# q and k in products of 512 columns, a smaller step of side work beside them, and a third Strassen piece in the second down product

## The chip, the cores and the metric

The kernel runs on one core of a Trainium2 chip. The metric is the device time of one execution in microseconds (us). The engines have short names in the profile: PE is TensorE's matrix products and PEld its weight loads (they overlap), DVE is VectorE, ACT is ScalarE, POOL is GpSimd, SP is SyncE, from whose queue the large loads are started.

## The reference, cut to what matters

One decoder layer on a sequence of 256 tokens with 1024 channels, all in float32:

```
h = h + 0.5 * rmsnorm(swiglu(rmsnorm(h)))                 # FFN 1: 1024 -> 2816 -> 1024
u = rmsnorm(h)
z, xbc, dt_raw, q, k, v, gate_logits = split(u @ w_in)
y_ssd = ssd_branch(z, xbc, dt_raw)                        # Mamba-2: conv, 2 chunks of 128, gated norm, @ ssd_w_branch
y_att = diff_attn_branch(q, k, v)                         # 8 heads, two softmaxes each, norm, @ da_w_branch
h = h + rmsnorm((gates[0] * y_ssd + gates[1] * y_att) @ w_out)
h = h + 0.5 * rmsnorm(swiglu(rmsnorm(h)))                 # FFN 2, of the same form
```

with `swiglu(x) = (silu(x @ w_gate) * (x @ w_up)) @ w_down`. Of q, k and v, head h has q and k as two halves of 64 channels and one v of 128; its output is `softmax(q0 k0) v - lam * softmax(q1 k1) v`, normed over its 128 channels.

## The kernel before

**Products in three terms.** Operands are split into two parts that TensorE multiplies in one pass each: hi (a cast by ACT) and lo (what is left, a subtraction by DVE). A product is hi x hi + hi x lo + lo x hi, so each weight chunk costs ACT a cast and DVE a subtraction per 1024 columns (`split_steps`, L249 and L252), and TensorE three matmuls per block of 128 x 128.

**Weights.** All weights arrive as chunks of 1 MB through a ring of three buffers (`raw`, loads from SP's queue at L228). A buffer's next load is issued when the chunk in it has been split. `take()` hands out the next chunk and has the splits of up to three chunks ahead put into the program. The split parts, and most other large tiles, share a pool of 29 buffers of 4 KB per partition (`k4`); a smaller one (`k3`) has four.

**Forms of a product.** `mm_t` (L293) gives 256 output channels by 256 tokens in one PSUM tile: 48 matmuls of 256 columns. `mm_w` (L305) gives the same in two tiles of 128 channels; hi weights multiply the hi and lo activations at once, 512 columns, lo weights the hi activations, 256 columns: 16 matmuls of each kind. ACT then copies one half of the tile and DVE adds the other (L318, L319). Gate and up of both FFNs use `mm_w`; B, C, x, z, q and k of the mixer use `mm_t`. `natural` (L1352) is the form with tokens on the partitions: per chunk two groups of 12 matmuls of 512 columns, one for each block of 128 tokens. PSUM tiles of products come from a ring of three (`pj`).

**Down product.** `mm_quads` sums the hidden layer in pieces. A plain piece `p` is one chunk of 256 hidden channels, 24 matmuls of 512 columns. A piece `q` is two chunks by Strassen's algorithm (in Winograd's form): seven products of six matmuls where two plain pieces have 48 matmuls. Four of its seven weight operands are sums that DVE forms (`Quad.sum_of`, L121), each of the seven is then cast (L129) and subtracted (L134); `sums_of` (L603 and on) forms the activation sums while gate and up still run. `DOWN` gives the order of pieces, the digit being the pair of chunks; `FIRST` and `LAST` the order of the seven products in all `q` but the last, and in the last. When the last `q` is through, four additions (L649) combine the Strassen sums, and the three plain pieces at the end are done block by block (`mm_n`, L568), so that the first block's norm lies beside the second block's products.

**Side work of the mixer.** SSD steps and attention are written as generators that yield after each step with a cost in us that is written by hand. `Background.run(us)` adds `us` to a due time and emits steps until it is used up, or until a step yields `BREAK`. The calls stand between the products of the projections: `run(0.4)` after each x chunk, `run(BG_US)` with 3.15 after each z, q and k chunk, `run(GATE_US)` (1.35) after each group of 12 gate products (`pgt`), `run(SSD_US)` (1.55) after each group of the SSD branch product (`pws`) and of the first half of the attention branch product (`pwd`). The queue holds, one behind the other, the causal B-C products, four SSD groups, four SSD norms (their sum over channels is the two matmuls `pn`), and attention.

Attention goes by pairs of heads. A step of it emits scores (`psc`, L1161), softmax (L1168 and on), the turns of the pair before (`pa`, L1196), its values (`po`, L1208 to L1210), its norm (square on ACT L1222, reduction on DVE L1224, root on ACT, scaling on DVE L1229), and the turn of the normed output of the pair before that (`pto`, L1235), whose hi and lo parts (L1247, L1248) are the operands of `pwd`. Before `pwd` begins, steps are emitted until pairs 0 and 1 are turned; after the first chunk of `pwd`, `attended` emits all that is left.

**Order.** From the gate products on, TensorE's instructions stand in the order in which they are written (`own_order(PE)`); the order on ACT and DVE there, and on all engines in the projections and in gate and up, comes from a scheduler. Each engine takes its instructions in order, and the loads of SP's queue are started in order.

Of the kernel before, what the change touches and what calls it, by code (L numbers as in the profile page):

```python
# [17 lines left out]
F32R = mybir.dt.float32r  # L18
AF = mybir.ActivationFunctionType
ALU = mybir.AluOpType  # L20
# [6 lines left out]
P = 128  # L27
T = 256
# [13 lines left out]
FILL = 2  # L42
TAIL = 3
BG_US = 3.15
GATE_US = 1.35
SSD_US = 1.55
DOWN = {"f1": "p q1 p p q2 p ppp", "f2": "p q1 p p q2 p ppp"}
FIRST, LAST = (1, 2, 3, 5, 7, 6, 4), (1, 6, 7, 2, 5, 3, 4)
BREAK, STOP = object(), object()

# [2 lines left out]
def tile_hybrid_layer(ctx: ExitStack, tc: tile.TileContext, x, ffn1_pre_g, ffn1_w_gate, ffn1_w_up,  # L53
# [4 lines left out]
    nc = tc.nc  # L58
# [5 lines left out]
    def k4(shape, name, dt=F32):  # L64
        return sb.tile(shape, dt, tag="k4", name=name, bufs=K4_BUFS)

    def k3(shape, name, dt=F32):
        return sb.tile(shape, dt, tag="k3", name=name, bufs=K3_BUFS)

    def k2(shape, name, dt=F32):  # L70
        return sb.tile(shape, dt, tag="k2", name=name, bufs=K2_BUFS)
# [7 lines left out]
    def pj(name):  # L79

        return ps.tile([P, 512], F32, tag="pj", name=name, bufs=3)

    def pjt(name):

        return pj(name).rearrange("p (m t) -> p m t", m=2)

    def bg(shape, name):
        return ps.tile(shape, F32, tag="bg", name=name, bufs=5)
# [3 lines left out]
    class Quad:  # L92
# [32 lines left out]
        def split(self, p):  # L125
            load_to(self.i + 2)
            hi = k4([P, 2, 512], f"wqh{self.i}{p}", F32R)
            src = self.quarter(self.PLAIN[p], p) if p in self.PLAIN else self.sum_of(p)
            nc.scalar.copy(hi, src)  # L129
            for later in self.products[self.products.index(p) + 1:][:1]:  # L130
                if later in self.SUMS:
                    self.sum_of(later)
            lo = k4([P, 2, 512], f"wql{self.i}{p}", F32R)
            last_lo[0] = nc.vector.tensor_sub(lo, src, hi.bitcast(F32)).ins  # L134
            self.give_back()
            return lambda kt: hi[:, kt, :], lambda kt: lo[:, kt, :]
# [28 lines left out]
    down, QUADS = {}, {}  # L165
    for tag, plan in DOWN.items():
        QUADS[tag] = [int(c) for c in plan if c.isdigit()]
# [90 lines left out]
    def split_to(n):  # L258

        while len(splits) < min(n, len(units)):  # L260
            of, p = units[len(splits)]
            if p is not None:
                splits.append(of.split(p))
                continue
            for _ in split_steps():
                pass

    def ahead_of(i, n):

        n *= 4  # L270
        while n > 0 and i < len(units):
            n -= 4 if units[i][1] is None else 1
            i += 1
        return i

    def take(ahead=AHEAD):

        i = taken[0]
        taken[0] += 1
        split_to(ahead_of(i, ahead))  # L280
        (of, p), w = units[i], splits[i]
        splits[i] = None
        if p is not None:
            return w
        his, los = w
        nj = chunks[of][1][1] // 2
        return (lambda j: his[j // nj][:, j % nj, :], lambda j: los[j // nj][:, j % nj, :])
# [5 lines left out]
    def mm_t(acc, w, act, k0=0, first=True, last=True, ks=range(KD)):  # L293

        (wh, wl), (ah, al, _) = w, act
        acc = acc if isinstance(acc, list) else [acc[:, m, :] for m in range(2)]
        for m in range(2):
            cs = slice(m * P, (m + 1) * P)
            for j in ks:
                nc.tensor.matmul(acc[m], wh(j)[:, cs], ah(k0 + j), start=first and j == ks[0], stop=False)  # L300
                nc.tensor.matmul(acc[m], wh(j)[:, cs], al(k0 + j), start=False, stop=False)  # L301
            for j in ks:
                nc.tensor.matmul(acc[m], wl(j)[:, cs], ah(k0 + j), start=False, stop=last and j == ks[-1])

    def mm_w(dst, name, w, act):  # L305


        (wh, wl), (ah, _, ahl) = w, act
        for m in range(2):
            acc = pj(f"{name}{m}")  # L310
            cs = slice(m * P, (m + 1) * P)
            for j in range(KD):
                if j:
                    nc.tensor.matmul(acc[:, :T], wl(j)[:, cs], ah(j), start=False, stop=False)  # L314
                nc.tensor.matmul(acc, wh(j)[:, cs], ahl(j), start=j == 0, stop=j == KD - 1)  # L315
                if not j:
                    nc.tensor.matmul(acc[:, :T], wl(j)[:, cs], ah(j), start=False, stop=False)
            nc.scalar.copy(dst[:, m, :], acc[:, T:])  # L318
            nc.vector.tensor_tensor(dst[:, m, :], acc[:, :T], dst[:, m, :], ALU.add)  # L319

    def mm_nat(acc, w, act, k0, first, last, late):

# [26 lines left out]
    def act_table(name):  # L349
        f = nc.scalar.preload_act_table_set(name)  # L350
        for prev in act_since:
            tc.add_manual_dep(f.ins, prev, order, reason="activation table")
        act_since.clear()
        act_fence[0] = f.ins.name
# [61 lines left out]
    for name, v in (("mx", mix_pre_g), ("f2", ffn2_pre_g),  # L416
                    ("ng", ssd_norm_g), ("cb", ssd_conv_b), ("sg", da_subln_g)):
        n = v.shape[1] // P
# [7 lines left out]
    def new_u(tag):  # L426
        for i in range(2):
            uT[i] = sb.tile([P, 4, 2, T], F32R, tag="u8", name=f"u{i}_{tag}", bufs=2)

    act_u = (lambda j: uT[j // 4][:, j % 4, 0, :], lambda j: uT[j // 4][:, j % 4, 1, :],  # L430
             lambda j: uT[j // 4][:, j % 4, :, :])
# [163 lines left out]
    def sums_of(g, even, odd):  # L595


        bs = (slice(0, P), slice(P, T))
        v = k4([P, 4, 2, P], f"sv{g}")
        hi, lo = (k3([P, 3, 2, P], f"s{n}{g}", F32R) for n in "hl")  # L600
        more = k2([P, 2, 2, P], f"s4{g}", F32R)
        nc.vector.tensor_tensor(v[:, 0], even[:, :, bs[1]], odd[:, :, bs[1]], ALU.add)
        nc.vector.tensor_sub(v[:, 2], even[:, :, bs[0]], even[:, :, bs[1]])  # L603
        nc.vector.tensor_sub(v[:, 1], v[:, 0], even[:, :, bs[0]])
        nc.vector.tensor_sub(v[:, 3], odd[:, :, bs[0]], v[:, 1])
        split(hi, lo, v[:, 0:3])
        split(more[:, 0], more[:, 1], v[:, 3])
        return ([hi[:, i] for i in range(3)] + [more[:, 0]], [lo[:, i] for i in range(3)] + [more[:, 1]])
# [417 lines left out]
    for i in range(4):  # L1026
        acc = pjt(f"pbc{i}")
        mm_t(acc, take(), act_u)
        dst = (bT, cT)[i // 2]
# [111 lines left out]
    qT = [None] * 2  # L1141
    kT = [None] * 2
# [167 lines left out]
    back = Background()  # L1310
    back.add(cb_work())
    for g in range(4):
        xs[g] = k4([P, 4, T], f"xs{g}")
        for i in range(2):
            acc = pjt(f"pxs{g}{i}")
# [5 lines left out]
    for g in range(4):  # L1321
        sz[g] = k4([P, 4, T], f"sz{g}")
        for i in range(2):
            acc = pjt(f"pz{g}{i}")
            mm_t(acc, take(), act_u)
            nc.scalar.copy(sz[g][:, i * 2:i * 2 + 2, :], acc)
            back.run(BG_US)
    act_table(SILU)
# [4 lines left out]
    for c in range(4):  # L1333
        if c % 2 == 0:
            qT[c // 2] = k4([P, 4, T], f"q{c}")
            kT[c // 2] = k4([P, 4, T], f"k{c}")
        o = (c % 2) * 2
        acc = pjt(f"pq{c}")
        mm_t(acc, take(), act_u)
        nc.scalar.activation(qT[c // 2][:, o:o + 2, :], acc, AF.Copy, scale=0.125)  # L1340
        back.run(BG_US)
        acc = pjt(f"pk{c}")
        mm_t(acc, take(), act_u)
        nc.scalar.copy(kT[c // 2][:, o:o + 2, :], acc)
        back.run(BG_US)

    back.add(att_work())

# [3 lines left out]
    def natural(name, n, hi, lo, evict, us, then=lambda: None):  # L1352


        accs = [pj(f"{name}{b}") for b in range(2)]
        for i in range(n):
            w = take()
            for b in range(2):
                bs = slice(b * P, (b + 1) * P)
                mm_nat(accs[b], w, (lambda k: hi(k)[:, bs], lambda k: lo(k)[:, bs]), i * 4, i == 0, i == n - 1, "u")  # L1360
                if i == n - 1:
                    evict(b, accs[b])
                back.run(us)
            if i == 0:
                then()
# [9 lines left out]
    for half in range(2):  # L1375
# [4 lines left out]
        for q in range(2):  # L1380
            def gate(b, acc):
                nc.vector.tensor_tensor(gt[half][b][:, halves[q]], acc, gb[:, halves[q]], ALU.add)

            natural(f"pgt{half}{q}", 2, uh, ul, gate, GATE_US)
    opens.append(open_gates)
# [42 lines left out]
    acc = [[bg([P, 512], f"acc_mx{b}{q}") for q in range(2)] for b in range(2)]  # L1428
# [47 lines left out]
```

## Time and profile before

| | us |
|---|---|
| median of 3 runs (lowest to highest) | 739.85 (739.61 to 741.19) |
| the profiled execution | 740.56 |
| its span, first to last instruction | 738.9 |
| DVE's most costly group: lo parts of weights (L252) | 271.1 in 230 instructions |
| ACT's: hi parts of weights (L249) | 229.9 in 229 |
| matmuls of gate and up, 512 columns (L315) | 2 x 288 instructions |
| q and k products, on PE | from 344.7 to 398.0 |
| down product of FFN 2, on PE | from 674.24 to 732.0 |

In rows of grouped instructions stand line, engine, operation, output <- inputs, sizes, count, then busy time and the mean of one in ns, and the idle time ahead of them with what ended it. In the timeline's rows stand start, duration in us, engine, line, operation, names and count; in brackets the idle time ahead and what ended it. In rows by stage, each engine has its busy time and, in parentheses, its number of instructions; then the granted TensorE clock, the share of the DMA engines and GB/s.

### The profile page before, as it was taken

The numbers are of one execution on the slowest core, as the hardware profiler recorded it, in microseconds if no ns is written. First come the engines' busy times: TensorE is split into PE (matmuls) and PEld (weight loads), VectorE is DVE, ScalarE is ACT, GpSimd is POOL, SyncE is SP. The second block draws the span as 40 slices with busy tenths as digits, with TensorE's granted clock in tenths as the row PEclk, the third lists the DMA queues.
The fourth block names the chain that finished last, engine by engine and source line by source line (L and its number), as shares of the span: only waits on it lengthen the run. The fifth ranks groups of instructions, "written<-read, shape, count | busy, mean of one in ns | idle before, by whom it ended". The sixth has DMA issues, their size and how long they took to land.

```text
span 738.9 us, 11097 instructions
## 1 busy us (share of the span) xinstructions
PE 729.9 (99%) x4345; PEld 637.2 (86%) x4345; DVE 576.5 (78%) x875; ACT 456.1 (62%) x764; POOL 38.8 (5%) x72
## 2 busy tenths in 40 slices
PE   8999999999999999999999999999999999999996
PEld 7888888888889999999999888888888888888884
DVE  6978768998677888777878997685784878768964
ACT  6657556665566565959957656782663656656542
POOL 2700000000300000000000000000010000000000
PEclk9999999999999999999999999999999999999998
DMA  8884674469353647566556556475471764843641
GB/s 291 234 256 150 221 229 171 159 201 355 119 172 116 202 140 231 187 192 220 172 162 213 168 175 211 126 237 190 127 238 35 228 206 152 270 170 128 214 143 57
DMA packets 94212, 137.96 MB, mean 187 GB/s; under 512 B 2684, under 2 KB 68304, under 8 KB 94160
## 3 DMA queue, kind: packets, MB, share of 16 engines
q1 hardware_dynamic: 91488, 129.51, 53.8%
q0 software_dynamic: 2368, 7.22, 3.2%
q8 instruction: 34, 0.56, 0.3%
q10 hardware_dynamic: 304, 0.53, 0.2%
q14 instruction: 18, 0.15, 0.1%
HBM read 136.17 MB, written 1.08 MB: 186 GB/s over the span
## 4 chain that ended last, share of the span: by engine, by line
PE 99%; DMA 0%; DVE 0%; ACT 0%; DVEq 0%; issue 0%
PE pup_f L315 9%; PE pg_f L315 9%; PE pws L330 6%; PE pgt L330 6%; PE acc_f2p L620 5%; PE acc_f1p L620 5%; PE pg_f L314 4%; PE pup_f L314 4%; PE pn_f L340 3%; PE pn_f L330 3%; PE acc_mx L568 3%; PE pn_mx L330 3%; PE pwd L330 3%; PE acc_f1p L568 3%; PE acc_f2p L568 3%; PE pz L301 2%
## 5 line engine op out<-in xcount | busy, mean ns | idle before, releaser
L252 DVE TENSOR_TENSOR wlo<-raw,whi 128x1024 fp32r<-128x1024 f32 (+1 forms) x230 | 271.1, 1209 | 27.3 <-ACT whi L249 26.0
L249 ACT CAST whi<-raw 128x1024 fp32r<-128x1024 f32 (+1 forms) x229 | 229.9, 1044 | 24.4 <-PE pgt L330 5.8
L315 PE MATMUL pg_f<-u_f,whi 128*128 128x512 f32 x288 | 101.3, 396 | 0.0
L315 PE MATMUL pup_f<-u_f,whi 128*128 128x512 f32 x288 | 101.1, 396 | 0.0
L314 PE MATMUL pg_f<-u_f,wlo 128*128 128x256 f32 x252 | 70.6, 280 | 0.0
L314 PE MATMUL pup_f<-u_f,wlo 128*128 128x256 f32 x252 | 70.3, 279 | 0.0
L315 PEld LDWEIGHTS pg_f<-u_f,whi 128*128 128x128 f32 x288 | 52.8, 188 | 9.7
L315 PEld LDWEIGHTS pup_f<-u_f,whi 128*128 128x128 f32 x288 | 52.7, 188 | 9.8
L314 PEld LDWEIGHTS pg_f<-u_f,wlo 128*128 128x128 f32 x252 | 47.5, 189 | 1.8
L314 PEld LDWEIGHTS pup_f<-u_f,wlo 128*128 128x128 f32 x252 | 47.5, 189 | 1.6
L319 DVE TENSOR_TENSOR su_f<-pup_f,su_f 128x256 f32<-128x256 f32 x36 | 15.1, 421 | 26.7 <-ACT su_f L318 26.7
L318 ACT COPY su_f<-pup_f 128x256 f32<-128x256 f32 x36 | 13.3, 371 | 32.7 <-PE pup_f L315 32.6
L330 PE MATMUL pgt<-whi,u_mx 128*128 128x512 f32 x128 | 33.1, 393 | 0.0
L300 PE MATMUL pxs<-u_mx,whi 128*128 128x256 f32 x128 | 31.7, 285 | 0.0
L301 PE MATMUL pz<-u_mx,whi 128*128 128x256 f32 x128 | 31.7, 284 | 0.0
L300 PE MATMUL pz<-u_mx,whi 128*128 128x256 f32 x128 | 31.6, 284 | 0.0
L301 PE MATMUL pxs<-u_mx,whi 128*128 128x256 f32 x128 | 31.4, 283 | 0.0
L129 ACT CAST wqh<-wt 128x1024 fp32r<-128x1024 f32 x16 | 16.8, 1052 | 23.5 <-DVE wt L121 22.3
L330 PEld LDWEIGHTS pgt<-whi,u_mx 128*128 128x128 f32 x128 | 23.6, 188 | 5.4 <-DVE yl L291 0.3
L1004 DVE SCALAR_TENSOR_TENSOR xs<-pxs,cols_b,xs 128x255 f32<-128x255 f32 (+2 forms) x48 | 21.9, 476 | 6.3 <-ACT xs L1001 5.9
L301 PEld LDWEIGHTS pz<-u_mx,whi 128*128 128x128 f32 x128 | 24.5, 192 | 0.2 <-issue 0.2
L301 PEld LDWEIGHTS pxs<-u_mx,whi 128*128 128x128 f32 x128 | 24.5, 192 | 0.0
(395 smaller groups left out, 1677.2 us busy)
## 6 DMA issues: line engine op xcount, KB each, us to landing
raw<-in_w_in_dram SPq DMA_DIRECT2D x40, 1024.0 KB, 5.5
raw<-in_ffn_w_down_dram SPq DMA_DIRECT2D x22, 1024.0 KB, 5.0
raw<-in_ffn_w_gate_dram SPq DMA_DIRECT2D x20, 1024.0 KB, 5.6
raw<-in_ffn_w_up_dram SPq DMA_DIRECT2D x20, 1024.0 KB, 5.5
raw<-in_ssd_w_branch_dram SPq DMA_DIRECT2D x8, 1024.0 KB, 5.1
acb<-acd POOLq DMA_DIRECT2D x8, 512.0 KB, 5.4
raw<-in_da_w_branch_dram SPq DMA_DIRECT2D x4, 1024.0 KB, 5.3
raw<-in_w_out_dram SPq DMA_DIRECT2D x4, 1024.0 KB, 5.1
```

The costliest lines, as they stand in the source:

```text
L129: nc.scalar.copy(hi, src)
L249: copy(hi[:, js, :], r[:, q * nj + j:q * nj + j + n, :])
L252: nc.vector.tensor_sub(lo[:, js, :], r[:, q * nj + j:q * nj + j + n, :], hi[:, js, :].bitcast(F32))
L300: nc.tensor.matmul(acc[m], wh(j)[:, cs], ah(k0 + j), start=first and j == ks[0], stop=False)
L301: nc.tensor.matmul(acc[m], wh(j)[:, cs], al(k0 + j), start=False, stop=False)
L314: nc.tensor.matmul(acc[:, :T], wl(j)[:, cs], ah(j), start=False, stop=False)
L315: nc.tensor.matmul(acc, wh(j)[:, cs], ahl(j), start=j == 0, stop=j == KD - 1)
L330: nc.tensor.matmul(acc, a(k0 + j), b(j), start=first and i == 0, stop=last and i == 11)
L340: nc.tensor.matmul(accs[b], x_(k0 + j), w_(j), start=first and j == 0 and w_ is wh and x_ is acts[b][0], stop=last and j == 3 and w_ is wl)
L568: nc.tensor.matmul(acc[b][q], x_[:, ts], w_(kt)[:, halves[q]], start=begin and i == 0 and kt == 0 and x_ is ah and w_ is wh, stop=i == n - ...
L620: nc.tensor.matmul(bank[p], x_, w_, start=p not in begun, stop=last and p in (1, 5, 6, 7))
L1004: nc.vector.scalar_tensor_tensor(dst[:, m, s:], acc[:, m, :T - s], cw(3 - s, c), dst[:, m, s:], ALU.mult, ALU.add)
```

## The change

Three edits go together. q and k are computed by `mm_w` in place of `mm_t` (q's scale of 0.125 is taken into both halves of the eviction). After each of their eight chunks the side work is given `QK_US`, 2.4, in place of `BG_US`, 3.15. In the second FFN's down product a third pair of chunks goes by Strassen's algorithm, and the order of pieces is `q1 p q2 p q3 ppp` in place of `p q1 p p q2 p ppp`; the activation sums of that third piece take their two buffers from the pool `k4`, since `k3` has only four.

```diff
+QK_US = 2.4
...
-DOWN = {"f1": "p q1 p p q2 p ppp", "f2": "p q1 p p q2 p ppp"}
+DOWN = {"f1": "p q1 p p q2 p ppp", "f2": "q1 p q2 p q3 ppp"}
...
-    def mm_w(dst, name, w, act):
+    def mm_w(dst, name, w, act, scale=None):
...
-            nc.scalar.copy(dst[:, m, :], acc[:, T:])
-            nc.vector.tensor_tensor(dst[:, m, :], acc[:, :T], dst[:, m, :], ALU.add)
+            if scale is None:
+                nc.scalar.copy(dst[:, m, :], acc[:, T:])
+                nc.vector.tensor_tensor(dst[:, m, :], acc[:, :T], dst[:, m, :], ALU.add)
+            else:
+                nc.scalar.activation(dst[:, m, :], acc[:, T:], AF.Copy, scale=scale)
+                nc.vector.scalar_tensor_tensor(dst[:, m, :], acc[:, :T], scale, dst[:, m, :], ALU.mult, ALU.add)
...
-        hi, lo = (k3([P, 3, 2, P], f"s{n}{g}", F32R) for n in "hl")
+        hi, lo = ((k3 if g < 3 else k4)([P, 3, 2, P], f"s{n}{g}", F32R) for n in "hl")
...
-        acc = pjt(f"pq{c}")
-        mm_t(acc, take(), act_u)
-        nc.scalar.activation(qT[c // 2][:, o:o + 2, :], acc, AF.Copy, scale=0.125)
-        back.run(BG_US)
-        acc = pjt(f"pk{c}")
-        mm_t(acc, take(), act_u)
-        nc.scalar.copy(kT[c // 2][:, o:o + 2, :], acc)
-        back.run(BG_US)
+        mm_w(qT[c // 2][:, o:o + 2, :], f"pq{c}", take(), act_u, 0.125)
+        back.run(QK_US)
+        mm_w(kT[c // 2][:, o:o + 2, :], f"pk{c}", take(), act_u)
+        back.run(QK_US)
```

## Prediction, made before the changed kernel was run

> **What bounds the kernel now.** I read first the page's busy shares and its chain, then busy time by stage, then TensorE's timeline in the stages that the change touches, and last what ScalarE and VectorE do beside it.
>
> ```profile
> PE 729.9 (99%) x4345; PEld 637.2 (86%) x4345; DVE 576.5 (78%) x875; ACT 456.1 (62%) x764; POOL 38.8 (5%) x72
> ...
> PE 99%; DMA 0%; DVE 0%; ACT 0%; DVEq 0%; issue 0%
> ```
>
> TensorE (PE) is busy 99% of the span and is 99% of the chain that ended last. So a matmul taken out shortens the kernel, and a wait put ahead of a matmul lengthens it: hardly any idle time is there to absorb one. By stage (q and k; the attention branch product; gate and up of the second FFN; the Strassen part of its down product):
>
> ```profile
> core 0: us, PE busy (x) PEld busy (x) DVE busy (x) ACT busy (x) POOL busy (x), PEclk, DMA share, GB/s
> 345.00:398.00 53.00, 53.00 (x460) 51.24 (x459) 42.71 (x62) 41.46 (x67) 1.34 (x3) 1.00 0.56 174
> ...
> 503.20:526.00 22.80, 22.80 (x107) 18.94 (x106) 10.54 (x14) 5.56 (x7) 0.53 (x1) 1.00 0.25 78
> 574.00:674.00 100.00, 100.00 (x575) 87.15 (x575) 77.75 (x106) 63.12 (x97) 0.00 (x0) 1.00 0.61 200
> 674.20:710.00 35.80, 35.80 (x157) 29.32 (x156) 33.13 (x33) 21.48 (x24) 0.63 (x1) 1.00 0.62 217
> ```
>
> Everywhere PE is full. VectorE (DVE) is busy 33.13 of 35.8 us in the down stage, so it is the engine that has least to give there; in the attention branch product it is nearly idle, since all side work is done by then. That will matter.
>
> **Edit 1: q and k by 512 columns.** One chunk of 256 outputs was 48 products of 256 columns; it becomes 16 of 512 and 16 of 256, the form that gate and up already use. TensorE's timeline has both forms:
>
> ```profile
> 386.52 0.28 PE L300 MATMUL pq<-u_mx,whi 128*128 128x256 f32 x1
> ...
> 392.27 0.28 PE L300 MATMUL pk<-u_mx,whi 128*128 128x256 f32 x1
> ...
> 663.05 0.40 PE L315 MATMUL pg_f<-u_f,whi 128*128 128x512 f32 x1
> ...
> 668.64 0.40 PE L315 MATMUL pup_f<-u_f,whi 128*128 128x512 f32 x1
> ...
> 674.24 0.62 PE L620 MATMUL acc_f2p<-whi,gh_f 128*128 128x512 f32 x2
> ```
>
> The old chunk takes 392.27 - 386.52 = 5.75 us, the new form 5.59 and 5.60. Eight chunks: 8 x 0.155 = **1.25 us saved**, all on the path. [...]
>
> Each chunk is evicted in two halves by ScalarE (ACT) and a DVE addition in place of one ACT copy.
>
> ```profile
> L319 DVE TENSOR_TENSOR su_f<-pup_f,su_f 128x256 f32<-128x256 f32 x36 | 15.1, 421 | 26.7 <-ACT su_f L318 26.7
> ```
>
> That is 16 x 0.42 = 6.7 us of DVE in a stage where 10.3 of 53 us are free; an evicted PSUM tile has two further tiles of 2.8 us each before its buffer is wanted. I cost it at nothing; if that cover were gone, each late eviction would stop PE by its own 0.4 us, at most 16 x 0.4 = 6.7.
>
> **Edit 2: the spacing.** `QK_US` 2.4 for 3.15 lets the planner emit 8 x 0.75 = 6.0 us (its own costs) less side work between q and k products. The work is not gone: it moves later. In the built program the sums of the last two SSD norms move from behind the first and second group of 12 gate products to behind the fifth and seventh, the first attention scores come after nine such groups instead of five, and the end of attention is pushed out of the SSD branch product. TensorE's order there is fixed by the kernel. Before, as the trace shows it:
>
> ```profile
> 491.41 0.39 PE L1210 MATMUL po<-v,aT 128*128 128x128 f32 x2
> 491.64 0.60 PE L1235 MATMUL pto<-ident,o 128*128 128x128 f32 x4
> ...
> 496.60 0.39 PE L1210 MATMUL po<-v,aT 128*128 128x128 f32 x2
> ...
> 499.60 0.60 PE L1235 MATMUL pto<-ident,o 128*128 128x128 f32 x4
> 499.95 1.18 PE L330 MATMUL pws<-whi,yh 128*128 128x512 f32 x4
> ...
> 502.81 0.60 PE L1235 MATMUL pto<-ident,o 128*128 128x128 f32 x4
> 503.16 1.18 PE L330 MATMUL pwd<-whi,oh 128*128 128x512 f32 x4
> ```
>
> Values of pair 3 (L1210, 496.60), 24 `pws` products with a turn between, then its turn (502.81). In the changed program the `pws` products have run out: values of pair 2, turn of pair 1, 12 `pwd`, turns of heads 6 and 7, 12 `pwd`, values of pair 3, turn of pair 2, **turn of pair 3**, the rest of `pwd`. What the turn of pair 3 waits for is shown by pair 2 in the trace:
>
> ```profile
> 489.82 1.05 ACT L249 CAST whi<-raw 128x1024 fp32r<-128x1024 f32 x1 [1.40 <-DMA raw<-in_da_w_branch_dram]
> 491.84 0.60 ACT L1222 ACTIVATE o<-po 128x512 f32<-128x512 f32 x1 [0.97 <-PE po L1210]
> 492.33 0.68 ACT L1247 ACTIVATE oh<-pto,g 128x512 fp32r<-128x512 f32 x1
> 493.92 0.44 ACT L357 ACTIVATE ro<-ro 128x4 f32<-128x4 f32 x2 [0.15 <-DVE ro L1225]
> ...
> 492.47 0.69 DVE L1224 TENSOR_REDUCE ro<-o 128x4 f32<-128x512 f32 x1 [0.34 <-ACT o L1222]
> 493.07 0.74 DVE L1248 SCALAR_TENSOR_TENSOR ol<-pto,g,oh 128x512 fp32r<-128x512 f32 x1
> 494.39 0.69 DVE L1229 TENSOR_TENSOR o<-po,ro 128x512 f32<-128x512 f32 x1 [0.51 <-ACT ro L357]
> ```
>
> Square (491.84), reduction, root, scaling (ends 495.08): 3.28 us from the last value product's end (491.80), the neighbour pair's split (0.74) in it, as it will be again.
> - *Stall b*, turn of pair 3: 3.28, plus 0.16 until that product's end (491.80 less the next start, 491.64), less the one turn that PE has meanwhile (499.95 - 499.60 = 0.35): **3.1 us**; without the 0.74 in it 2.4.
> - *Stall c*, right behind: a turn lands after 0.60, ACT's scaling into hi takes 0.68, and PE has 0.35 and two products (2 x 0.227) of its own: **0.5**.
> - *Stall a*, at the first `pwd`: it wants pair 1, whose turn stands directly ahead of it. With ACT free: Square of pair 2 (0.49 to the next start) and hi (0.68) after po's end, 1.2 + 0.16 - 0.35 - 0.45 = 0.6 us. But ACT takes its work in order, and ahead of these two stands the cast of a weight chunk that waits for its load, as the row at 489.82 did for 1.40. Top: 0.6 + 1.40 + 1.05 (the cast) = 3.0. The rows beside it are the same queue, so I take nearer the top, **2.3**.
>
> Queued behind PE's waits is only `pwd` and everything after it; nothing later catches up, PE being full to the end. The loads' queue (SP) keeps its order.
>
> **Edit 3: a third Strassen piece in f2.** Seven products for eight: 42 in place of 48 matmuls of 512 columns.
>
> ```profile
> 674.40 35.77 PE acc_f2p L620 x156
> 710.17 21.79 PE acc_f2p L568 x96
> ```
>
> 6 x 35.77/156 = **1.38 us saved**. Price, on DVE: four weight sums and three more splits (7 x 1.135, from the next rows), and in gate and up four activation sums (0.42 each, as the row of L319) and their split (1.135), 2.8 us, hidden by the 22 us that DVE has free there. ACT's casts (1.05) are shorter than DVE's part and lie beside it.
>
> ```profile
> 659.39 2.35 DVE L252 TENSOR_TENSOR wlo<-raw,whi 128x1024 fp32r<-128x1024 f32 x2
> ...
> 673.46 1.22 DVE L134 TENSOR_TENSOR wql<-wt,wqh 128x1024 fp32r<-128x1024 f32 x1
> 674.60 0.75 DVE L319 TENSOR_TENSOR su_f<-pup_f,su_f 128x256 f32<-128x256 f32 x2
> ...
> 676.81 0.69 DVE L291 TENSOR_TENSOR gl_f<-sg_f,gh_f 128x512 fp32r<-128x512 f32 x1 [0.74 <-ACT gh_f L290]
> ...
> 680.83 2.50 DVE L134 TENSOR_TENSOR wql<-wt,wqh 128x1024 fp32r<-128x1024 f32 x2
> 683.25 4.63 DVE L252 TENSOR_TENSOR wlo<-raw,whi 128x1024 fp32r<-128x1024 f32 x4
> ...
> 690.76 1.23 DVE L121 TENSOR_TENSOR wt<-raw,wt 128x1024 f32<-128x1024 f32 x1 [1.75 <-DMA raw<-in_ffn_w_down_dram]
> ```
>
> Four in 4.63 us, so 1.135 each. A piece costs DVE 11 x 1.135 = 12.5 us against 42 x 0.227 = 9.5 of PE; pieces now stand with one plain chunk between. Walk DVE's queue from the first down product, t0 (674.24). From the second operation of the row at 659.39 to that at 673.46, eight were done on down weights by t0. Eight again leave three of piece 1 and two of the chunk, 5.7; the last up eviction, product and split, 2.8 (674.60 to their end at 677.4, with the wait); piece 2, the chunk, and ten operations of piece 3, 23 x 1.135 = 26.1: t0 + 34.6. Only then is the buffer free for the last chunk's load.
>
> ```profile
> raw<-in_ffn_w_down_dram SPq DMA_DIRECT2D x22, 1024.0 KB, 5.0
> ```
>
> Landed 39.6, cast 40.7, split 41.9. PE wants it after 174 + 12 products: 186 x 0.227 = 42.2. Under 1 us of margin: a wait such as the 1.75 in the rows goes straight through. Between 0 and 2.5 us (two such waits); I take **1.0**.
>
> **Sum.** -1.25 - 1.38 + 2.3 + 3.1 + 0.5 + 1.0 = **+4.3 us**. The profiled execution took 740.56 (span 738.9), the median of three 739.85; on the median, **744.2**. Low ends of the terms give +0.9, high ends +6.5.
>
> **Rivals.**
> - *The clock falls too.* The last matmul ends at 710.17 + 21.79 = 732.0; behind it the granted clock (PEclk) shows:
>
> ```profile
> 734.00:735.00 1.00, 0.00 (x0) 0.00 (x0) 0.98 (x2) 0.00 (x0) 0.00 (x0) 0.76 0.00 0
> 735.00:736.00 1.00, 0.00 (x0) 0.00 (x0) 0.43 (x1) 0.00 (x0) 0.00 (x0) 0.50 0.35 133
> ```
>
> A mean of 0.76 in that microsecond puts the fall to half at 734.5: 2.5 us of idleness were enough, and stall b is 3.1. Half speed lasted from there to the end of the span, 4.4 us; as long again under `pwd` costs 2.2: +6.5, **746.4**. Against it: other gaps are short. [...] Chance 0.25.
> - *Faster.* The norm of pair 3, at the last turn, is done while PE still has `pwd` products, because the queues of ACT and DVE are empty by then (DVE works 10.54 of 22.8 us in that stage); with no stall left the gain stands, -2.6, **737.2**. It decides once all stalls together are under 1.1 us (2.6 less 1.5). Against it: the 3.28 of the chain is its own length, not queueing. Chance 0.05.
> - *Near nothing.* No cast ahead of stall a, b at 2.4, no wait in the down product: +0.9, **740.8**. Chance 0.08.
> - *The q and k form does not pay*, its evictions or weight loads being late (PEld 51.24 of 53): 1.25 not gained, 745.5. Chance 0.04.
>
> **How the numbers follow.** Forecast 0.58, the rivals as given. The forecast's own range is 740.8 to 746.4, the clock rival's 2.2 higher, to 748.6; 741.0 to 747.8 leaves out the fringes and the faster case, no more than 2 in 10. A run here tells 0.2% (1.5 us) from no change: faster 0.05, same 0.08, slower 0.87.
>
> **What would show it.** Right: PE idle at the first `pwd` (on ACT), at the last `pto` (on DVE, about 3 us) and in the last down chunk; q and k chunks of 5.6 us; 246 down products. Wrong: no PE idle between 480 and 520, or `pto` of pair 3 ahead of `pwd`.

## Result and profile after

The changed kernel took 745.46 us (median of 4 runs, 743.69 to 746.04) against 739.79 for the kernel before: a ratio of 1.007 (95% interval 1.0057 to 1.0082), 5.7 us slower. Six more runs, in a second series, gave 744.74 against 739.91, 1.0067 (1.0055 to 1.0079). The profiled execution took 745.50, its span 743.8; the one before took 740.56, its span 738.9. Lines of the changed kernel stand up to five higher than those of before (L335 is `mm_nat`, L1240 the turn, L625 and L573 the down product, L253 and L250 the splits).

Busy shares and chain of the page, for the changed kernel:

```profile
PE 729.8 (98%) x4211; PEld 630.1 (85%) x4211; DVE 591.3 (80%) x904; ACT 461.7 (62%) x777; POOL 38.8 (5%) x72
...
PE 91%; DVE 4%; ACT 2%; DMA 1%; issue 1%; SPq 0%; DVEq 0%; ACTq 0%
```

There are 134 matmuls fewer and 29 VectorE instructions more. TensorE's busy time is the same to 0.1 us (which is itself a sign: fewer products, but some of them slow), and 9% of the chain's length lies off TensorE. What TensorE waited for, in the view of its waits (us in total, times, longest):

```profile
PE pto L1240 <- DVE o L1234: 3.0, 1, 3.0
...
PE pwd L335 <- ACT oh L1252: 1.6, 1, 1.6
PE pwd L335 <- ACT o L1252: 0.3, 1, 0.3
...
PE acc_f2p L573 <- DVE wlo L253: 0.2, 1, 0.2
```

All four are the waits that the prediction named; the others are 1.6 us at the kernel's start, as in the kernel before, and two of 0.2. Here the four stand in TensorE's timeline:

```profile
498.66 0.71 PE L335 MATMUL pwd<-whi,oh 128*128 128x512 f32 x2
500.96 0.73 PE L335 MATMUL pwd<-whi,oh 128*128 128x512 f32 x2 [1.59 <-ACT oh L1252]
...
508.10 0.60 PE L1240 MATMUL pto<-ident,o 128*128 128x128 f32 x4
511.69 0.63 PE L1240 MATMUL pto<-ident,o 128*128 128x128 f32 x4 [2.99 <-DVE o L1234]
512.07 0.71 PE L335 MATMUL pwd<-whi,o 128*128 128x512 f32 x2
513.10 1.01 PE L335 MATMUL pwd<-whi,o 128*128 128x512 f32 x2 [0.31 <-ACT o L1252]
513.91 1.91 PE L335 MATMUL pwd<-wlo,o 128*128 128x512 f32 x4
...
723.54 0.40 PE L573 MATMUL acc_f2p<-whi,gl_f 128*128 128x512 f32 x1
724.11 0.50 PE L573 MATMUL acc_f2p<-wlo,gh_f 128*128 128x512 f32 x1 [0.17 <-DVE wlo L253]
```

The number in brackets counts idle time from the modelled end of the last product. What a wait costs is read from start to start instead, less the work that lies between: 500.96 - 498.66 - 2 x 0.227 = 1.85 us (a), 511.69 - 508.10 - 0.35 = 3.24 (b), 513.10 - 512.07 - 2 x 0.227 = 0.58 (c), 724.11 - 723.54 - 0.23 = 0.34 (d). Each is 0.2 to 0.3 above its bracket. Most of that is overlap: in an unbroken stream a product starts 0.23 us after the one before, while its row lasts 0.39, and the bracket counts only from the row's end. Below, this extra time is called the restart.

The row at 513.91 shows something more: four products in 1.91 us, where before they take 1.07. The granted clock (PEclk, third number from the end) in windows of 1 us:

```profile
512.00:513.00 1.00, 0.79 (x5) 0.35 (x3) 0.00 (x0) 0.76 (x2) 0.00 (x0) 1.00 0.03 12
513.00:514.00 1.00, 0.90 (x3) 0.72 (x4) 0.75 (x1) 0.04 (x1) 0.00 (x0) 0.68 0.00 0
514.00:515.00 1.00, 1.00 (x4) 0.81 (x3) 0.00 (x0) 0.00 (x0) 0.00 (x0) 0.50 0.00 0
515.00:516.00 1.00, 1.00 (x3) 0.76 (x3) 0.00 (x0) 0.00 (x0) 0.00 (x0) 0.50 0.00 0
516.00:517.00 1.00, 1.00 (x4) 0.81 (x3) 0.00 (x0) 0.00 (x0) 0.00 (x0) 0.61 0.00 0
517.00:518.00 1.00, 1.00 (x6) 0.79 (x5) 0.69 (x1) 0.00 (x0) 0.00 (x0) 1.00 0.00 0
```

If the clock is either full or half, a mean of 0.68 puts the fall to half at 513.36, and 0.61 the return at 516.78: 3.42 us at half clock, 1.71 us of work lost. The clock rival happened.

**Where the 4.9 us of span came from.** The stage borders in both timelines, first the kernel before (q, gates, output product, last product of the second down product), then the changed one:

```profile
344.77 0.28 PE L300 MATMUL pq<-u_mx,whi 128*128 128x256 f32 x1
...
398.03 0.63 PE L330 MATMUL pgt<-whi,u_mx 128*128 128x512 f32 x2
...
525.95 0.62 PE L568 MATMUL acc_mx<-whi,mh 128*128 128x512 f32 x2
...
731.55 0.39 PE L568 MATMUL acc_f2p<-wlo,gh_f 128*128 128x512 f32 x1
```

```profile
344.61 0.40 PE L316 MATMUL pq<-u_mx,whi 128*128 128x512 f32 x1
...
396.60 0.63 PE L335 MATMUL pgt<-whi,u_mx 128*128 128x512 f32 x2
...
531.64 0.62 PE L573 MATMUL acc_mx<-whi,mh 128*128 128x512 f32 x2
...
736.49 0.39 PE L573 MATMUL acc_f2p<-wlo,gh_f 128*128 128x512 f32 x1
```

q and k: 53.26 to 51.99, **-1.27**. Gates to the end of the attention branch product: 127.92 to 135.04, **+7.12**; waits a, b, c and the half clock are 1.85 + 3.24 + 0.58 + 1.71 = 7.38, which is 0.26 more than that. From there to the last product: 205.60 to 204.85, **-0.75**. The sum is +5.1; the start of q, 0.16 earlier, makes it the 4.9 of the spans.

### The profile page after: what moved, and what is told of

The parts are those of the page before. It is cut to its first block, busy times and chain, and to the rows that moved or that the text cites. A ratio compares the mean times of both kernels' runs of the same rounds, so it can differ in the third digit from the quotient of the medians.

```text
span 743.8 us, 10863 instructions
## 1 busy us (share of the span) xinstructions
PE 729.8 (98%) x4211; PEld 630.1 (85%) x4211; DVE 591.3 (80%) x904; ACT 461.7 (62%) x777; POOL 38.8 (5%) x72
## 4 chain that ended last, share of the span: by engine, by line
PE 91%; DVE 4%; ACT 2%; DMA 1%; issue 1%; SPq 0%; DVEq 0%; ACTq 0%
PE pup_f L316 9%; PE pg_f L316 9%; PE pgt L335 6%; PE acc_f1p L625 5%; PE pg_f L315 4%; PE pup_f L315 4%; PE pws L335 4%; PE pwd L335 3%; PE pn_f L345 3%; PE pn_mx L335 3%; PE pn_f L335 3%; PE acc_mx L573 3%; PE acc_f1p L573 3%; PE acc_f2p L625 2%; PE pz L302 2%; PE pxs L304 2%
## 5 line engine op out<-in xcount | busy, mean ns | idle before, releaser
L253 DVE TENSOR_TENSOR wlo<-raw,whi 128x1024 fp32r<-128x1024 f32 (+1 forms) x226 | 266.6, 1208 | 21.6 <-ACT whi L250 21.0
L250 ACT CAST whi<-raw 128x1024 fp32r<-128x1024 f32 (+1 forms) x225 | 226.0, 1044 | 21.4 <-DMA raw<-in_w_in_dram 4.0
L130 ACT CAST wqh<-wt 128x1024 fp32r<-128x1024 f32 x20 | 21.1, 1053 | 23.7 <-DVE wt L122 23.7
L335 PE MATMUL pgt<-whi,u_mx 128*128 128x512 f32 x128 | 32.8, 392 | 0.0
L335 PEld LDWEIGHTS pgt<-whi,u_mx 128*128 128x128 f32 x128 | 23.7, 188 | 5.4 <-DVE yl L292 0.3
L135 DVE TENSOR_TENSOR wql<-wt,wqh 128x1024 fp32r<-128x1024 f32 x20 | 24.4, 1219 | 0.2
```

The source lines that it names most:

```text
L250: copy(hi[:, js, :], r[:, q * nj + j:q * nj + j + n, :])
L253: nc.vector.tensor_sub(lo[:, js, :], r[:, q * nj + j:q * nj + j + n, :], hi[:, js, :].bitcast(F32))
L335: nc.tensor.matmul(acc, a(k0 + j), b(j), start=first and i == 0, stop=last and i == 11)
```

## Experiments

Theory: the spacing makes the whole loss, by waits a, b and c and the half clock behind b; the other two edits gain a little. Rivals: the down product's new order, with VectorE full there (31.79 of 33 us), makes a part of it, or the evictions of q and k do. The first four kernels take the change apart.

**Spacing undone.** In the changed kernel:

```diff
-QK_US = 2.4
+QK_US = 3.15
```

> The changed kernel with QK_US back at 3.15: 512 columns for q and k and the third Strassen piece stay. Theory (the spacing alone makes the loss: three waits of 1.59, 2.99 and 0.31 us in the attention branch product, and some 1.7 us of half clock behind the second): all of them go and the two gains stand, 739.8 - 1.25 - 1.38 + 0.2 = 737.3 us. Rival (the down product's new order, with VectorE full there, makes a good part of the loss): no better than 740. Rival (the 16 more VectorE additions of q and k are late): no better than 739.8.

Measured: 738.51 against 740.05, ratio 0.9976 (0.9964 to 0.9988), 1.5 us faster than before. Its waits of TensorE:

```profile
PE warm L411 <- POOL ident L397: 1.6, 1, 1.6
PE pu_mx L456 <- DVE h L550: 0.9, 1, 0.9
PE pn L1119 <- DVE ssum L292: 0.3, 1, 0.3
```

No wait at `pwd` or `pto` is left (the 0.9 at `pu_mx` lies ahead of every edit and in none of the next three profiles). Both rivals fall as causes of the loss, but the gain is 1.0 us short of the 2.5 expected. The two edits by themselves, below, show where most of that went.

**Spacing alone.** In the kernel before, `back.run(BG_US)` behind each q and k chunk:

```diff
-        back.run(BG_US)
+        back.run(2.4)
```

> The kernel before with one edit: 2.4 instead of 3.15 after each q and k chunk. Theory: the whole loss and none of the gains, 739.8 + 1.59 + 2.99 + 0.31 = 744.7 us without a fall of the clock, 746.4 with one of 1.7 us. Rivals (the loss comes from the down product or from q and k in 512 columns): 739.8, no change.

Measured: 747.49 against 740.05, 1.0094 (1.0073 to 1.0116), +7.4 us; a second series (below) gave +7.0. The spacing alone does the harm, and the sum that fits is the one with the fall of the clock: the start-to-start costs of a, b and c and 1.7 us make 7.4.

**512 columns alone.** The changed kernel with both other edits undone:

```diff
-QK_US = 2.4
+QK_US = 3.15
-DOWN = {..., "f2": "q1 p q2 p q3 ppp"}
+DOWN = {..., "f2": "p q1 p p q2 p ppp"}
```

> The changed kernel with QK_US at 3.15 and the old order of the second down product, so that only the 512 columns for q and k are left. Theory: eight chunks by 0.155 us, 739.8 - 1.25 = 738.55 us, and no wait on q or k evictions. Rival (the evictions by two engines are late): 739.8 or more.

Measured: 739.55 against 740.05, 0.9989 (0.9978 to 1.0001): -0.5, not told from no change. So the time alone doesn't refute the rival of late evictions; the profile does, for TensorE waits for no eviction of q or k in it. TensorE's timeline shows where some of the 1.25 went:

```profile
402.39 0.39 PE L1119 MATMUL pn<-ssum,ones_r 128*128 128x256 f32 x1 [0.27 <-DVE ssum L292]
```

With q and k done 1.3 us earlier, the sum of an SSD norm among the gates comes too soon for VectorE; the wait is new, and with the 0.2 to 0.3 of a restart, as at the waits above, it takes some 0.5 us back (an estimate). The changed kernel has no such wait, since its spacing moves these sums behind later gate groups. Another 0.4 lies outside the span: the runs of this kernel took 2.0 to 2.1 us more than their spans, those of every other kernel here 1.65 to 1.78. Why this kernel alone does so stays open.

**Third piece alone.** The kernel before with `"f2": "q1 p q2 p q3 ppp"` and the third piece's activation sums in tiles of their own:

```diff
-        hi, lo = (k3([P, 3, 2, P], f"s{n}{g}", F32R) for n in "hl")
+        hi, lo = ((k3 if g < 3 else k4)([P, 3, 2, P], f"s{n}{g}", F32R) for n in "hl")
```

> The kernel before with only the third Strassen piece in the second down product. Theory: six products of 0.23 us less and 0.2 us of waiting in the last chunk, 739.8 - 1.38 + 0.2 = 738.6 us. Rival (VectorE is the bound there and gives the gain back): 739.8 or more, with over 1 us of idle TensorE in the down product.

Measured: 739.28 against 740.05, 0.9985 (0.9972 to 0.9998): -0.8 for -1.2. The rows of before say why the gain itself is less than 1.38:

```profile
679.70 0.39 PE L620 MATMUL acc_f2p<-wqh,gh_f 128*128 128x512 f32 x1
...
689.38 0.62 PE L620 MATMUL acc_f2p<-whi,gh_f 128*128 128x512 f32 x2
```

A Strassen piece takes 9.68 us, 0.2305 for each of its 42 products; the plain chunk ahead of it (674.24 to 679.70) takes 5.46 for 24, 0.2275 each. Two plain chunks less one piece is 10.92 - 9.68 = 1.24. Less wait d, 0.34, that is 0.9.

**Time given back later.** The next three ran with the changed kernel on one chip.

> The changed kernel itself, on the same chip as the next three, for a direct comparison and a better median. All theories: 745 to 746 us (four runs so far gave 743.69 to 746.04).

Measured: 744.74 against 739.91 (six runs, 743.70 to 746.48).

```diff
-GATE_US = 1.35
+GATE_US = 1.65
```

> The changed kernel with GATE_US 1.65 in place of 1.35: sixteen gate groups may emit 0.3 us more each, 4.8 of the 6.0 us that the narrower spacing of q and k took away. Theory (only that attention ends after the SSD branch product costs time, not the narrower spacing itself): the waits at pwd and pto vanish although QK_US stays 2.4, and the time is that of the spacing undone or a little less, 738.0 to 738.5. Rival (side work among q and k matmuls is worth more than later): 740 to 745.

Measured: 737.84 against 739.91, 0.9973 (0.9961 to 0.9984), -2.1 us. The narrow spacing of q and k is harmless as soon as the gates take its work: what costs is only that attention ends too late. Against the kernel before of its own series it is also 0.5 better than the kernel with the spacing undone; the wait at `pn`, worth about that much, is not in its profile.

Then the third piece one chunk further from the end, beside GATE_US 1.65:

```diff
-"f2": "q1 p q2 p q3 ppp"
+"f2": "q1 p p q2 p q3 pp"
```

> As the kernel with GATE_US 1.65, and the second down product in the order q1 p p q2 p q3 pp, so that the third piece is two chunks from the end and its weights have one more chunk's time. Theory: the wait of 0.2 us and its restart in the last chunk go as well, 0.3 us less than the kernel with GATE_US 1.65, so 737.7 to 738.2, below both kernels. Rival (the wait moves to the third piece): equal to it.

Measured: 737.66 against 739.91, 0.9971 (0.9961 to 0.9981), -2.2 us, the fastest version here. Its TensorE waits for nothing but the kernel's start:

```profile
PE warm L411 <- POOL ident L397: 1.6, 1, 1.6
PE pu_f L456 <- DMA h<-in_x_dram: 0.4, 2, 0.2
```

Wait d is gone, but 0.2 us apart the two times can't be told from each other.

**The half clock by itself.** The changed kernel, with ten products ahead of the last turn:

```diff
             pt = bg([P, 4, P], f"pto{hp}")
+            for _ in range(10 if hp == 3 else 0):
+                nc.tensor.matmul(pt[:, 0, :], ident, ident, start=True, stop=True)
```

> The changed kernel with ten matmuls of ident by ident added ahead of the turn of pair 3, into the tile that this turn then overwrites. They add no result; they keep TensorE at work in the 3.0 us in which it waits (four of this kind took 1.06 us at the kernel's start, so ten take about 2.4). Theory (half clock follows the idle time and costs about 1.7 us): the wait ends where it did, the granted clock stays at 1.00 behind it, and the time is 1.7 us below the changed kernel's, 743.8. Rival (the clock falls for another reason, or the half clock costs nothing): the same time as the changed kernel, 745.5, with PEclk of 0.5 behind the turn.

Measured: 744.63 against 739.91, 1.0062 (1.0049 to 1.0074): no better than the changed kernel. The profiled execution was a long one, 749.52. In it the clock stayed up behind the turn, but fell behind wait a (1.76 us idle there), and near the kernel's start TensorE waited 1.3 us for a split of weights. The mean granted clock of this execution is 0.993; the half clock behind wait a (3.40 us) and the one at the end (from 743.48 on, 4.3 us) alone would leave 0.995 of its 747.8 us, so one more fall is likely, an estimate. Its first `pwd` comes 2.77 us later than in the second profile of the same kernel (500.98 against 498.21), and the turn of pair 2 4.61 later (512.23 against 507.62). So the same kernel was run again, and beside it one that fills wait a too:

```diff
+            for _ in range(6 if name == "pwd0" and i == 0 else 0):
+                nc.tensor.matmul(accs[0][:, :P], ident, ident, start=True, stop=True)
```

> The kernel with ten idle-time matmuls ahead of the turn of pair 3 once more. Its time was 744.6, no better than the changed kernel (744.7), and its one profile was 5 us longer than its other runs, with PEclk of 0.5 not behind the turn of pair 3 but behind the first wait at pwd (1.76 us idle). Theory A (half clock follows idle time, and with the second wait filled it now falls behind the first one): PEclk of 0.5 for some 3 us behind the first pwd wait, none behind the turn, 744.5 us. Theory B (the fall of the clock was never worth 1.7 us): PEclk of 1.00 throughout the stage and still 744.5.

> As that kernel, and six more matmuls of ident by ident ahead of the first pwd product, into the accumulator that this product then starts anew; they fill some 1.4 of the 1.6 us of the first wait. Theory A: PEclk of 1.00 in the whole stage and 743.0 to 743.8 us, 1 to 1.7 below the changed kernel (744.7). Theory B: no change, 744.5.

Measured: 744.74 (ten products) and 745.02 (sixteen) against 740.56: 1.0052 (1.0036 to 1.0067) and 1.0052 (1.004 to 1.0065). Theory A's account fails: PEclk is 1.00 in the whole attention branch product of both, and still the times stand where they did. But theory B fails too, because the stage is shorter: from the waiting turn to the output product 18.4 us in both (511.12 to 529.5 with ten products) against 511.69 to 531.64 = 19.95 in the changed kernel. The time is lost again later. With ten products, ScalarE's and TensorE's timelines at the second down product show:

```profile
667.95 1.05 ACT L130 CAST wqh<-raw 128x1024 fp32r<-128x1024 f32 x1 [3.60 <-DMA raw<-in_ffn_w_down_dram]
```

```profile
676.81 0.47 PE L316 MATMUL pup_f<-u_f,whi 128*128 128x512 f32 x1 [1.24 <-DVE sg_f L321]
```

The cast of the first piece's weights waited 3.60 us for its load (2.28 in the second profile of the changed kernel); VectorE's queue behind it was late for the up product, and TensorE stood still for 1.24. With sixteen products the same happens with the last chunk's load (2.88 against 1.40), and TensorE waits three times there, 1.15 in all. Chance is not a likely cause for the first: both profiles of the kernel with ten products show the wait at the up product (1.24 us here, 1.4 in the long one), and neither of the changed kernel's does (its casts waited 2.20 and 2.28 for the load). Why these loads come late there stays open. So the last pair puts the same ten products where VectorE and the loads have time in hand, in the kernel with the spacing alone and the old down product:

> The kernel before with the narrower spacing alone, once more, on the same chip as the next one. All theories: some 7.4 us above the kernel before, as in its first run, with PEclk of 0.5 for some 3 us behind the turn of pair 3.

> The kernel before with the narrower spacing and the ten matmuls of ident by ident ahead of the turn of pair 3, but the old second down product, in which VectorE and the loads have time in hand. Theory A (half clock costs 1.7 us of the stage, and where the gain did not show in the time the tight new down product took it back): PEclk of 1.00 behind the turn, 1.3 to 1.7 us below the kernel without the ten matmuls. Theory B (the half clock is not worth that): the same time as it.

Measured: 747.11 without and 745.81 with the ten products, against 740.09: 1.0099 (1.0084 to 1.0114) and 1.0085 (1.0065 to 1.0105). The medians are 1.3 us apart, the intervals overlap. The stage, without:

```profile
512.04 0.63 PE L1235 MATMUL pto<-ident,o 128*128 128x128 f32 x4 [2.99 <-DVE o L1229]
...
531.95 0.61 PE L568 MATMUL acc_mx<-whi,mh 128*128 128x512 f32 x2
```

```profile
514.00:515.00 1.00, 1.00 (x4) 0.79 (x3) 0.17 (x1) 0.00 (x0) 0.00 (x0) 0.52 0.00 0
515.00:516.00 1.00, 1.00 (x4) 0.81 (x3) 0.00 (x0) 0.00 (x0) 0.00 (x0) 0.50 0.00 0
```

and with them:

```profile
513.03 0.66 PE L1237 MATMUL pto<-ident,o 128*128 128x128 f32 x4 [0.67 <-DVE o L1229]
...
531.40 0.61 PE L568 MATMUL acc_mx<-whi,mh 128*128 128x512 f32 x2
```

```profile
514.00:515.00 1.00, 0.68 (x3) 0.48 (x3) 0.56 (x1) 0.41 (x1) 0.00 (x0) 1.00 0.00 0
515.00:516.00 1.00, 1.00 (x6) 0.78 (x5) 0.19 (x1) 0.00 (x0) 0.00 (x0) 1.00 0.00 0
```

19.91 against 18.37 us: the half clock costs 1.54 us of the stage. That much the profiles show. That it is worth as much in the time of the whole kernel, the medians make likely and the intervals leave open.

## Why the prediction was right, and where it was off

The forecast was 744.2 us, slower at 0.87; the time is 745.46 (744.74 in the second series), inside the range. By its steps:

| step | forecast us | measured us |
|---|---|---|
| q and k in 512 columns | -1.25 | -1.27 |
| third piece | -1.38 | -1.24 |
| a, first `pwd` | +2.3 | +1.85 |
| b, turn of pair 3 | +3.1 | +3.24 |
| c, `pwd` behind it | +0.5 | +0.58 |
| d, last down chunk | +1.0 | +0.34 |
| sum | +4.3 | +3.5 |
| half clock (a rival, 0.25) | +2.2 | +1.5 to 1.7 |

The measured rows add up to 5.0 to 5.2; the profiled executions differ by 4.9, the medians by 5.7 and by 4.8.

*q and k.* Right in the changed kernel. Alone it does not show in the time: there some 0.5 goes to the norm sums that the shorter chunks overtake, and 0.4 lies outside the span. The prediction had read that the spacing moves these sums, and had not asked what they do without it.

*Third piece.* Off by 0.14: the mean of 156 products mixed two rates, and the piece's own products are the slower ones. The 1.24 comes from the rows of before. In the changed kernel a plain chunk takes 5.44 us and the second and third piece 9.69 and 9.57, which makes it 1.2 and 1.3.

*a.* The mechanism is right, the size too high. ScalarE in the changed kernel:

```profile
498.78 1.05 ACT L250 CAST whi<-raw 128x1024 fp32r<-128x1024 f32 x1 [2.31 <-DMA raw<-in_w_out_dram]
499.73 0.59 ACT L1227 ACTIVATE o<-po 128x512 f32<-128x512 f32 x1
500.22 0.68 ACT L1252 ACTIVATE oh<-pto,g 128x512 fp32r<-128x512 f32 x1
```

The cast stands ahead and waits for its load, as said, but most of that wait lies before TensorE gets there: the cast starts 0.12 us after the first `pwd` (498.66). The 0.6 of a free ScalarE and the cast's 1.05 remain, 1.65, and hardly any of the 1.40 of load wait that the top held.

*b and c.* As worked out from pair 2, with the neighbour's split (509.53) in the chain, to 0.14 and 0.08 us. VectorE in the changed kernel:

```profile
508.93 0.69 DVE L1229 TENSOR_REDUCE ro<-o 128x4 f32<-128x512 f32 x1 [4.79 <-ACT o L1227]
509.53 0.74 DVE L1253 SCALAR_TENSOR_TENSOR o<-pto,g,o 128x512 fp32r<-128x512 f32 x1
...
510.85 0.69 DVE L1234 TENSOR_TENSOR o<-po,ro 128x512 f32<-128x512 f32 x1 [0.51 <-ACT ro L362]
```

*d.* VectorE's walk left 0.3 us of margin, and the split came 0.17 late. Nothing more went through, so the 1.0 was mis-sized. How thin the margin is, the kernel with sixteen products showed: there the load of the last chunk was late, and TensorE waited for 1.15 us.

*The clock.* This is the step that failed: the forecast took the clock to hold, at 0.58 against 0.25, although its own threshold, 2.5 us of idleness, lay below its own wait, 3.1. "Other gaps are short" says nothing about this one. The threshold was itself the reading of one fall: in six profiles (the kernel before, the changed one and the spacing alone twice each, and the first with ten products) the clock fell 2.6 us after the last matmul in two and 3.9 to 5.2 us after it in four, and 3.1 lies between, so such a wait could bring a fall and did not have to. The rival's 746.4 had too long a half clock (4.4 us, cut off by the span's end; here 3.4) and was too high by that and by a and d. That the number came out within 1.3 us is luck, owed to two errors against each other: the waits and gains 0.8 too dear in the sum, the clock 1.6 too cheap.

## What to carry to other kernels

Where a planner spreads side work, count where its budget ends: work taken out of one stage comes out in a later one, and it costs nothing until its last chain stands ahead of the engine that is full (here, 4.8 us of budget given back among the gates turn +4.8 into -2.1). Price a new wait from start to start with the restart in it, by the same chain elsewhere in the trace, and if it is as long as the waits that brought a half clock here (2.99 us in four profiles, 1.76 in one; next section), put the lower clock into the forecast and not beside it. A gain of a few tenths per instruction is worked out from the rows of that instruction, not from a mean over two kinds.

## What the runs showed of the hardware

Amid the work the half clock came in blocks of one length. In the five profiles in which it fell in the attention branch product, it lasted 3.40 to 3.42 us each time by the fractions of PEclk (513.36 to 516.78 in the changed kernel). It did not come at once: there it fell 1.7 us after the wait had ended and products ran again, in the other four 0.9 to 2.0. In the 3.4 us ahead of the fall TensorE was busy for 1.4 us in the changed kernel: nothing up to 511, 0.31 in the microsecond from 511, 0.79 in the next, and 0.36 x 0.90 up to 513.36. And it was not tied to one size of wait: 2.99 us of idleness (wait b) brought it in all four profiles that show that wait, 1.76 us in one (wait a of the first kernel with ten products), while waits a of 1.31 to 1.64 us brought none in six others.

Within a profile, the distance from this fall to the one behind the last matmul repeats. Here is the fall behind the last matmul in the changed kernel, and then two falls of the long profile of the kernel with ten products:

```profile
742.00:743.00 1.00, 0.00 (x0) 0.00 (x0) 0.00 (x0) 0.00 (x0) 0.00 (x0) 0.53 0.01 2
```

```profile
504.00:505.00 1.00, 1.00 (x5) 0.79 (x4) 1.00 (x4) 0.40 (x2) 0.00 (x0) 0.78 0.98 406
...
743.00:744.00 1.00, 0.00 (x0) 0.00 (x0) 1.00 (x2) 0.00 (x0) 0.00 (x0) 0.74 0.00 0
```

In the changed kernel the falls are at 513.36 and 742.06, which is 228.70 us apart; in its second profile and in both of the spacing alone the distance is 228.68 to 228.70. In the other profile they are at 504.56 and 743.48, 238.92 apart: 10.22 more, which is three times 3.41, the length of a stretch at half clock. The last matmul ended 5.18 us ahead of the fall in the changed kernel and 2.58 ahead of it in the other. What decides whether a wait brings a fall, and when, was not shown. Two of the changed kernel's ten runs took 743.7 us, the others 744.5 to 746.5, and these two have the highest mean granted clock, 0.998 against 0.992 to 0.997. That fits two runs without a half clock amid the work, but they were not profiled.
